# An encoder of two layers in split precision: six seven-product pairs in w_out, five raw slots, an order of its own for each stage's first block

## The chip, the core and the metric

The kernel runs on one core of one Trainium2 chip. The metric is the device time of one execution in microseconds (us); lower is better. Three timed executions of the kernel before gave 2615.0, 2615.23 and 2615.27 us.

The engines are called as the profile calls them: PE (matmuls; PEld its weight loads), DVE (vector), ACT (scalar), POOL and SP. SP issues the loads of the weights, POOL the transfers of intermediate results and those that add to their destination.

## What is computed

The reference is a trunk of two layers over a sequence of 256 tokens of 4096 numbers, in float32. Each layer is

```python
h = rmsnorm(x, norm_w[l])
proj = h @ w_in[l]                      # 4096 x 11264
aq, ak, av, ag, rq, rk, rv, rg = jnp.split(proj, SPLIT_POINTS, axis=-1)
a_out = silu(ag) * gqa_attention(rope(rmsnorm(aq)), rope(rmsnorm(ak)), av)
r_out = silu(rg) * rmsnorm(bidirectional_retention(rope(rq), rope(rk), rv))
x = x + concat([a_out, r_out]) @ w_out[l]   # 4096 x 4096
```

and a last RMSNorm follows. The two projections are nearly all of the arithmetic.

## The kernel before

**Split products.** A float32 number is kept as the sum of two rounded parts, a high one and a low one. A product of two matrices is then three matmuls: high by high, low part of x by high, high by low part of the weight (`M<-whi,x8h`, `M<-whi,x8l` on line 1559, `M<-wlo,x8h` on line 1569). For the weights, ACT makes the high part (`whi<-wraw`, a cast) and DVE the low part (`wlo<-wraw,whi`, a subtraction). All recorded operations of DVE and ACT stand under line 267, a helper's.

**Blocks, pairs and pages.** A projection is done in blocks of 1024 output columns: 11 blocks for w_in and 4 for w_out in each layer. There are four stages: w_in and w_out of layer 0 (stages 0 and 1), then of layer 1 (2 and 3). In a block, the 4096 inputs are 16 pairs of 128-row slices. A pair is a 2 x 2 product of sub-matrices, done either as eight products or, after sums of the sub-matrices, as seven. `SEVENS` (line 85) says which pairs take seven: (3, 4, 6, 10, 11) for w_in and (4, 6, 10, 11, 12) for w_out. A pair of eight has two pages, A and B, each one weight tile of 128 x 1024 with four products. A pair of seven has four, A, T, B and U, with 2, 2, 1 and 2 products: T and U are sums that DVE forms (`wsum`), and B is half a tile (`bhi`, `blo`). Both kinds of pair load two tiles of 512 KB. A pair of seven holds both at once, until its sums and its half page are made.

**Buffers.** Raw weights come into `RAWS` = 6 slots (line 37). High and low parts of whole pages are in a ring of 5 (`RING`), half pages in 2. A load of a raw tile can start when a slot is free, that is, when DVE has read the tile before (`load`, line 483); a page can be cast when PE has released a place in the ring (`release`). 13 pages of 4 KB per partition serve everything else. The operand of x is kept for all 16 pairs: a pair that is ever one of seven has 7 x 128 numbers in `x7h` and `x7l`, the others 2 x 256 in `x8h` and `x8l`.

**Order.** The program is written out ahead by a planner in Python: it emits each engine's instructions in one fixed order, with a clock of its own (`Now`, `Clock`) that prices each operation by constants at the head of the file, and inserts the work between projections (attention, retention, rotary, splitting the next operand) where `Weights.room` (line 641) says that pages are far enough ahead. At run time each engine follows its list and waits on semaphores. Within a block the pairs go 0 to 15 in groups: a group begins with a pair of seven and takes the pairs of eight behind it, whose pages are put between those of the seven (`GROUPS`, `pages_of`). The first block of stage 0 alone has an order of its own, (1, 0, 2, 5, 3, 4, 7, 8, 9, 6, 10, 12, 13, 11, 14, 15), from `SPREAD`. Its pairs 1 and 0 are multiplied unsplit (line 1553) while the first weights come in.

**The end of a block.** Eight sums lie in PSUM; `combine` (line 1576) adds them on DVE into `ca` and `cb`. Where the planner has DVE more than `RELIEF` behind ACT, ACT copies a sum out first (`out`). For w_out the old x is then added by a transfer that accumulates (`ca<-in_x`, `cb<-in_x` on POOL), and the result is transposed for the next layer. The last block of the program has its own ending, `last_combine`.

**Transferred lows.** `far_parts` (line 562) can make a low part without DVE: ACT writes the high part and its negative, and a transfer from memory adds the weight to the negative. `FARS` (line 105) names the pairs whose page B is done so; it is empty before.

Of the kernel before, what the change touches and what calls it, by code (L numbers as in the profile page):

```python
# [14 lines left out]
ALU = mybir.AluOpType  # L15
# [18 lines left out]
BLK = 32  # L34
ALL = slice(None)
PAGES = 13
RAWS = 6

RING = 5
FAR = 1  # L40

STRICT = 9
RELIEF = 0.6
AHEAD = 5
SPARE = 2

HALVES = 2

STEP_V = 1.2
STEP_S = 1.5  # L50

V_FIXED = 0.1
S_FIXED = 0.16
# [2 lines left out]
PASS = 0.3  # L56

LANDING = 9.5
STORE = 5.0
FETCH = 13.0  # L60
FAR_LANDING = 9.0
MARGIN = 0.5

RUSH = 2.5

EARLY = 1.3

ADD_AHEAD = 3.0

NEED = {"ak": 4, "ag": 3, "rk": 5, "rg": 4}  # L70

PE_REST = 1.2

TIGHT_A = 2
TIGHT_B = 9

AT_ONCE = 3

WARM = 20

SPLITS = 1

START = 2

SEVENS = ((3, 4, 6, 10, 11), (4, 6, 10, 11, 12), (3, 4, 6, 10, 11), (4, 6, 10, 11, 12))

EVER = sorted(set(_p for _s in SEVENS for _p in _s))
EIGHTS = [_p for _p in range(NP) if _p not in EVER]
# [7 lines left out]
TAIL = (6, 5, 4)  # L96
LASTS = 2

HOLD = 4

NEAR = 40

LATE = 10

FARS = ((), (), (), ())


AQ, AK, AV, AG, RQ, RK, RVO, RG = 0, 2048, 2560, 3072, 5120, 6144, 7168, 9216
# [65 lines left out]
GROUPS = [  # L174
    ([tuple(range(_s[0]))] if _s[0] else []) + [tuple(range(_a, _b)) for _a, _b in zip(_s, _s[1:] + (NP,))] for _s in SEVENS
]
SPREAD = (4, 5, 9, 10, 13)
FIRST_ORDER = [1, 0] + [_p for _p in range(2, NP) if _p not in SEVENS[0]]
for _i, _p in zip(SPREAD, SEVENS[0]):
    FIRST_ORDER.insert(_i, _p)  # L180
FIRST_GROUPS = []
for _p in FIRST_ORDER:
    if _p in SEVENS[0] or not FIRST_GROUPS:
        FIRST_GROUPS.append(())
    FIRST_GROUPS[-1] += (_p,)
SHARED = ("M1", "M5", "M7", "M6")


# [39 lines left out]

TOGETHER = 4

OTHER = False

TURNS = "01"

# [47 lines left out]
def hybrid_encoder(  # L282
# [134 lines left out]
    class Weights:  # L417


        def __init__(self):  # L420
            self.pages = []
            for l in range(DEPTH):
                for w, n in ((w_in, N_IN), (w_out, N_OUT2)):
                    for b in range(n):
                        stage = 2 * l + (w is w_out)
                        start = (l, b) == (0, 0) and w is w_in
                        for g in FIRST_GROUPS if start else GROUPS[stage]:
                            for slot in slots_of(g, stage, start):
                                one = Page()
                                one.pair, one.kind, one.uses, one.left = slot[0][1], slot[0][3], len(slot), 3 * len(slot)  # L430
                                one.whole = start and one.pair in NATIVE
                                one.seven = one.pair in SEVENS[stage] and not one.whole
                                one.far = False
                                one.can = is_far(stage, one.pair, one.kind) and not (
                                    start and (one.pair < 6 or one.whole)
                                )
                                one.src, one.begun, one.low_at, one.next = [], False, None, []
                                one.kept, one.half = None, one.seven and one.kind == PAGE_B
                                one.allowed = one.wanted = False
# [325 lines left out]
    def split_operand(c, stage, rest=0.0):  # L765
        v, full[c] = full[c], None
        for k in range(2):
            p = 2 * c + k
            whole = None
            if stage == 0:  # L770
                whole = v.rearrange("p (k i n) -> p k i n", k=2, i=2)[:, k]
                w = v.rearrange("p (k i m a t) -> p k m i a t", k=2, i=2, m=MT, t=BLK)[:, k]
            else:
                w = v.rearrange("p (a m i t) -> p m i a t", a=4, m=MT, t=BLK)[:, :, 2 * k : 2 * k + 2]
            waiting.append(Lane(split_pair(p, w, whole, stage)))
            waiting[-1].pair, waiting[-1].ready = p, now.t + rest
        if stage == 0:
            waiting.sort(key=lambda v: (v.pair in NATIVE and not c, FIRST_ORDER.index(v.pair)))

    def split_late():  # L780
        split_operand(*late.pop(0))
# [74 lines left out]
    using = []  # L856

    spare, taken, window, want, users, last_block = {}, {}, [0, False, 99], [0], set(), [False]
    force = [False]

    def take_bank():

# [73 lines left out]
    def running():  # L936
# [4 lines left out]
            one.append(rest)  # L941
        return one

    def advance():

        clear()
        if not lanes + running():
            if waiting:
                split_step()
                return  # L950
            if turning and turning[0].step(True):
                return
            force[0] = True
        ready = lanes + running()
        force[0] = False
        if not ready:
            now.wait(now.t + 0.5)
            return
        one = min(ready, key=lambda v: v.ready)
        now.wait(one.ready)  # L960
        one.step()
        clear()

    def tick():

        weights.low_parts()
# [456 lines left out]
    def lead(stage):  # L1423

        return 8 * SEVENS[stage][0]

    def block(after_pair, phase, then, first_order=False, order=LAST_ORDER, last=None, hurried=False):

# [5 lines left out]
        flat = []  # L1434
        stage = phase - 1
        rush[0] = RUSH if hurried else 0.0
        for g in FIRST_GROUPS if first_order else GROUPS[stage]:
            for slot in slots_of(g, stage, first_order):
                flat += slot
        want[0] = 2  # L1440
# [58 lines left out]
            return a  # L1499

        opens = max(final[b] for b in SHARED)
        after = lead(then - 1) if then else 0

        def end_product(n, name, p, index, k, h):
            g = pages[p, k]
# [70 lines left out]
    def combine(bank, acc, c):  # L1576
# [15 lines left out]
        elif bank in ("M8", "M3", "M2", "M4"):  # L1592
            to = {"M8": cb[:, 1, :], "M3": cb[:, 0, :], "M2": ca[:, 0, :], "M4": ca[:, 1, :]}[bank]
            v = acc[bank]
            if not last_block[0] and ve.until - max(ac.until, now.t) > RELIEF and held[0] + pledged() < PAGES:
                v = page([P, NB], "out")
                ac.copy(v, acc[bank])
                drop()
            ve.tensor_add(to, to, v)

# [250 lines left out]
    for l, L in enumerate(layers):  # L1851
        for bi, (one, _) in enumerate(BLOCKS):
# [10 lines left out]
            c = block(after, 2 * l + 1, 2 * l + 1 + (bi == N_IN - 1), start)  # L1863
            ready = (lambda i=one[1], L=L: i in L.weights) if one[0] == "rg" else None
            tasks.append(Lane(in_task(L, *one, c), need=NEED[one[0]], own=2, gate=ready))
            if one[0] == "ag":
                users.update((v, l, one[1]) for v in "sv")
                tasks.append(Lane(attention_scores(L, one[1]), need=6, gate=lambda g=one[1], L=L: g in L.rs and now.t >= L.kept and near(LATE)))
# [5 lines left out]
        for n in range(N_OUT2):  # L1874
# [19 lines left out]
            else:  # L1894
                if final:
                    turning.append(Turn(2 * l + 2))
                c = block(after, 2 * l + 2, 2 * l + 2 + (n == N_OUT2 - 1), hurried=n == 0)
                tasks.append(Lane(out_tasks(l, n, c), need=4, own=2))


_INS = [
# [46 lines left out]
```

## Time and profile before

| | |
|---|---|
| timed executions, median | 2615.23 us (2615.0 to 2615.27) |
| profiled execution, its own time | 2615.02 us |
| its span, first to last instruction | 2613.2 us |
| outside the span | 1.8 us |
| granted clock of PE, mean | 0.998 |
| weight loads by SP | 956 of 512 KB |

The profile's page gives each engine's busy time. Views of the trace give instructions in order of time, the waits with what ended them, and the chain of work that ended last. The matmuls overlap in the record, so that one shows 389 ns while the next begins 227 ns after it: the pace is read from the starts, not from the durations. For DVE and ACT too the start of the next instruction in a full stretch tells what one costs.

### The profile page before, as it was taken

How to read it: one execution, taken by the hardware profiler on the slowest of the kernel's cores; microseconds unless marked ns; L12 is line 12 of the kernel's file. 1: busy time of each engine (PE TensorE's matmuls, PEld its weight loads, DVE VectorE, ACT ScalarE, POOL GpSimd, SP SyncE). 2: the span in 40 equal slices, each digit the busy share in tenths (PEclk: the TensorE clock that was granted, in tenths of full speed). 3: DMA queues.
4: the chain of work that ended last, by engine and by line, in shares of the span. 5: the costliest groups of instructions: out<-in, count | busy, mean ns of one | idle time of the engine just before them, and what ended most of it. 6: DMA issues, size and time to landing. Idle time of an engine off the chain costs nothing.

```text
span 2613.2 us, 33651 instructions
## 1 busy us (share of the span) xinstructions
PE 2599.5 (99%) x11650; PEld 2152.7 (82%) x11650; DVE 2283.5 (87%) x2715; ACT 1636.4 (63%) x2376; POOL 238.6 (9%) x368
## 2 busy tenths in 40 slices
PE   9999999999999999999999999999999999999998
PEld 7888888888888888888888888888888888888886
DVE  7998988998888998778998889988988798988777
ACT  7765766666555687555785566675665557765454
POOL 0010211111001000110001101210100010000000
PEclk9999999999999999999999999999999999999999
DMA  7876867876666666786777768777765676667774
GB/s 281 297 246 234 274 224 246 278 230 225 205 212 213 238 209 205 238 274 223 260 228 233 223 233 274 244 232 263 253 225 179 223 232 226 198 205 221 231 243 167
DMA packets 180667, 610.47 MB, mean 234 GB/s; under 512 B 21904, under 2 KB 28560, under 8 KB 180496
## 3 DMA queue, kind: packets, MB, share of 16 engines
q1 hardware_dynamic: 147040, 520.17, 59.4%
q0 software_dynamic: 32736, 87.05, 11.1%
q8 instruction: 91, 1.49, 0.2%
q10 hardware_dynamic: 720, 1.10, 0.1%
q14 instruction: 80, 0.66, 0.1%
HBM read 564.20 MB, written 44.04 MB: 233 GB/s over the span
## 4 chain that ended last, share of the span: by engine, by line
PE 97%; DVE 1%; issue 1%; ACT 1%; DMA 1%; SPq 0%; POOLq 0%; DVEq 0%; POOL 0%; ACTq 0%
PE M L1559 62%; PE M L1569 31%; PE M L1042 1%; PE M L1041 1%; PE M L1040 1%; PE M L1553 0%; DVE wlo L267 0%; DMA wraw<-in_w_in 0%; DMA whole<-in_w_in 0%; ACT whi L267 0%; DVE wsum L267 0%; DVE cb L267 0%; ACT ca L267 0%; DVE ca L267 0%; DVE x7l L267 0%
## 5 line engine op out<-in xcount | busy, mean ns | idle before, releaser
L267 ACT CAST whi<-wraw 128x1024 fp32r<-128x1024 f32 x806 | 835.5, 1047 | 555.8 <-PE M L1559 490.5
L267 DVE TENSOR_TENSOR wlo<-wraw,whi 128x1024 fp32r<-128x1024 f32 x806 | 965.2, 1214 | 129.5 <-ACT whi L267 127.5
L1559 PE MATMUL M<-whi,x8h 128*128 128x512 f32 x2368 | 922.1, 389 | 0.0
L1559 PE MATMUL M<-whi,x8l 128*128 128x512 f32 x2368 | 921.7, 389 | 0.0
L1569 PE MATMUL M<-wlo,x8h 128*128 128x512 f32 x2368 | 679.3, 389 | 0.0
L1559 PEld LDWEIGHTS M<-whi,x8h 128*128 128x128 f32 x2368 | 444.6, 188 | 92.1 <-issue 0.2
L1559 PEld LDWEIGHTS M<-whi,x8l 128*128 128x128 f32 x2368 | 444.6, 188 | 92.0 <-issue 0.2
L1569 PEld LDWEIGHTS M<-wlo,x8h 128*128 128x128 f32 x2368 | 442.8, 188 | 90.8
L267 ACT CAST whi<-wsum 128x1024 fp32r<-128x1024 f32 x300 | 315.5, 1052 | 227.9 <-DVE wsum L267 115.3
L1559 PE MATMUL M<-whi,x7h 128*128 128x512 f32 x1140 | 443.6, 389 | 0.0
L1559 PE MATMUL M<-whi,x7l 128*128 128x512 f32 x1140 | 443.5, 389 | 0.0
L267 DVE TENSOR_TENSOR wlo<-wsum,whi 128x1024 fp32r<-128x1024 f32 x300 | 365.5, 1218 | 27.0 <-ACT whi L267 26.6
L1569 PE MATMUL M<-wlo,x7h 128*128 128x512 f32 x1140 | 341.3, 389 | 0.3 <-DVE wlo L267 0.3
L1569 PEld LDWEIGHTS M<-wlo,x7h 128*128 128x128 f32 x1140 | 213.8, 188 | 45.2 <-DVE wlo L267 0.7
L1559 PEld LDWEIGHTS M<-whi,x7h 128*128 128x128 f32 x1140 | 214.0, 188 | 44.9 <-issue 0.4
L1559 PEld LDWEIGHTS M<-whi,x7l 128*128 128x128 f32 x1140 | 214.0, 188 | 44.4
L267 DVE TENSOR_TENSOR wsum<-wraw 128x1024 f32<-128x1024 f32 x150 | 182.4, 1216 | 1.5 <-DMA wraw<-in_w_in 1.5
L267 DVE TENSOR_TENSOR wsum<-wsum,wraw 128x512 f32<-128x512 f32 x150 | 103.8, 692 | 5.2
L267 DVE TENSOR_TENSOR wsum<-wraw,wsum 128x512 f32<-128x512 f32 x150 | 102.5, 684 | 0.6
L267 DVE TENSOR_TENSOR blo<-wraw,bhi 128x512 fp32r<-128x512 f32 x150 | 102.7, 685 | 0.0
L267 ACT CAST bhi<-wraw 128x512 fp32r<-128x512 f32 x150 | 92.3, 615 | 0.0
L267 DVE TENSOR_TENSOR cb<-cb,M 128x512 f32<-128x512 f32 x85 | 58.0, 682 | 37.5 <-PE M L1569 37.4
(223 smaller groups left out, 1876.6 us busy)
## 6 DMA issues: line engine op xcount, KB each, us to landing
wraw<-in_w_in SPq DMA_DIRECT2D x700, 512.0 KB, 4.5
wraw<-in_w_out SPq DMA_DIRECT2D x256, 512.0 KB, 4.2
full<-next_dram POOLq DMA_DIRECT2D x18, 512.0 KB, 7.4
kv<-kv_dram POOLq DMA_DIRECT2D x16, 512.0 KB, 7.0
p_dram<-room POOLq DMA_DIRECT2D x64, 128.0 KB, 3.6
pT<-p_dram POOLq DMA_DIRECT2D x16, 512.0 KB, 8.6
next_dram<-room POOLq DMA_DIRECT2D x40, 128.0 KB, 4.9
x<-in_x SPq DMA_DIRECT2D x8, 512.0 KB, 6.6
```

The costliest lines, as they stand in the source:

```text
L267: return call(out, *args, **kwargs)
L1040: nc.tensor.matmul(out, a[0], b[0], start=start, stop=False)
L1041: nc.tensor.matmul(out, a[0], b[1], start=False, stop=False)
L1042: nc.tensor.matmul(out, a[1], b[0], start=False, stop=stop)
L1559: nc.tensor.matmul(acc[name], a[i], g.hi[h], start=m == first[name] and not i, stop=False)
L1569: nc.tensor.matmul(acc[name], a, g.lo[h], start=False, stop=m == final[name])
```

## The change

- w_out takes seven products for pairs (4, 6, 7, 10, 11, 13), six in place of five; w_in keeps its five. Since a pair of x has its form for all stages, 7 tiles of `x7h` and `x7l` are held, and 9 of `x8h` and `x8l` (before 6 and 10).
- `RAWS` goes from 6 to 5.
- Each stage's first block has an order of its own (`opening_order`, `FIRST_GROUPS[stage]`). Stage 0: (1, 0, 2, 3, 4, 5, 7, 6, 8, 9, 12, 13, 10, 14, 11, 15). Stage 1: (0, 1, 2, 3, 5, 4, 6, 8, 7, 9, 10, 12, 11, 14, 13, 15). Stage 2: 0 to 15 as before. Stage 3: (0, 1, 2, 3, 5, 4, 6, 7, 8, 9, 10, 12, 11, 14, 13, 15).
- `FARS` names pair 15 in stage 1, pair 15 in stage 2, pairs 1 and 2 in stage 3. The planner uses nine of the pages: four in stage 1, two in stage 2, three in stage 3, each with a transfer `flo<-in_w_out` or `flo<-in_w_in` on POOL.
- `OTHER` = True: for the last two column blocks of a layer the transposed result goes to a page of its own (`to`).
- New values for the planner's constants. `ADDED` = 99 leaves the new transfer in `combine` unused.

```diff
-RAWS = 6
+RAWS = 5
...
-RELIEF = 0.6
-AHEAD = 5
-SPARE = 2
+RELIEF = 1.0
+ADDED = 99
+AHEAD = 4
+SPARE = 5
...
-STEP_S = 1.5
+STEP_S = 1.1
...
-STORE = 5.0
-FETCH = 13.0
-FAR_LANDING = 9.0
-MARGIN = 0.5
-RUSH = 2.5
+STORE = 7.0
+FETCH = 9.0
+FAR_LANDING = 10.0
+MARGIN = 0.8
+RUSH = 0.0
...
-ADD_AHEAD = 3.0
-NEED = {"ak": 4, "ag": 3, "rk": 5, "rg": 4}
+ADD_AHEAD = 1.5
+NEED = {"ak": 4, "ag": 3, "rk": 4, "rg": 5}
...
-AT_ONCE = 3
+AT_ONCE = 4
...
-START = 2
-SEVENS = ((3, 4, 6, 10, 11), (4, 6, 10, 11, 12), (3, 4, 6, 10, 11), (4, 6, 10, 11, 12))
+START = 1
+SEVENS = ((3, 4, 6, 10, 11), (4, 6, 7, 10, 11, 13), (3, 4, 6, 10, 11), (4, 6, 7, 10, 11, 13))
...
-HOLD = 4
+HOLD = 8
-LATE = 10
-FARS = ((), (), (), ())
+LATE = 35
+FARS = ((), (15,), (15,), (1, 2))
...
-SPREAD = (4, 5, 9, 10, 13)
-FIRST_ORDER = [1, 0] + [_p for _p in range(2, NP) if _p not in SEVENS[0]]
...
+SPREAD = (3, 4, 7, 12, 14)
+SPREAD1 = (5, 6, 8, 10, 12, 14)
+SPREAD2 = ()
+SPREAD3 = (5, 6, 7, 10, 12, 14)
+def opening_order(stage):
+    spread = (SPREAD, SPREAD1, SPREAD2, SPREAD3)[stage]
+    spread = spread if len(spread) == len(SEVENS[stage]) else SEVENS[stage]
+    order = [_p for _p in ([1, 0] if stage == 0 else [0, 1]) + list(range(2, NP)) if _p not in SEVENS[stage]]
+    for i, p in zip(spread, SEVENS[stage]):
+        order.insert(i, p)
+    return order
...
+FIRST_ORDER = [opening_order(_i) for _i in range(4)]
+FIRST_GROUPS = [grouped(_o, _i) for _i, _o in enumerate(FIRST_ORDER)]
+LEADS = [8 * next(_i for _i, _p in enumerate(_o) if _p in SEVENS[_s]) for _s, _o in enumerate(FIRST_ORDER)]
...
-OTHER = False
+OTHER = True
...
-        for g in FIRST_GROUPS if first_order else GROUPS[stage]:
+        for g in FIRST_GROUPS[stage] if opening else GROUPS[stage]:
...
-        after = lead(then - 1) if then else 0
+        after = 0 if not then else lead(then - 1) if then == phase else LEADS[then - 1]
...
-                c = block(after, 2 * l + 2, 2 * l + 2 + (n == N_OUT2 - 1), hurried=n == 0)
+                c = block(after, 2 * l + 2, 2 * l + 2 + (n == N_OUT2 - 1), opening=n == 0, hurried=n == 0)
```

Two places where the order of instructions moves. The first is DVE in the first block of stage 3 (w_out of layer 1), from the combination of the second retention head into `ca` (the sum in PSUM, M6, times `rst`, which POOL has prepared) on. `wsum` and `wlo` are sums and low parts of weights, `blo` a half page's; equal numbers mean the same tile. Before:

```order
L267 SCALAR_TENSOR_TENSOR ca_19656<-M6_20063,rst_20079,ca_19656 128x256 x2
L267 TENSOR_TENSOR wlo_20093<-wsum_20025,whi_20092 128x1024
L267 TENSOR_TENSOR blo_20096<-wraw_19898,bhi_20095 128x512
L267 STREAM_TRANSPOSE room_20110<-ca_19656 128x1024
L267 TENSOR_TENSOR wlo_20119<-wraw_19962,whi_20118 128x1024
L267 TENSOR_TENSOR wsum_20158<-wraw_19965,wraw_20007 128x1024
L267 TENSOR_TENSOR wlo_20145<-wsum_20087,whi_20144 128x1024
L267 TENSOR_TENSOR wsum_20191<-wraw_19965,wsum_20158 128x512
L267 TENSOR_TENSOR wsum_20191<-wsum_20191,wraw_20007 128x512
L267 TENSOR_TENSOR wlo_20161<-wraw_19965,whi_20160 128x1024
L267 TENSOR_TENSOR wlo_20181<-wraw_20055,whi_20180 128x1024
```

The same place in the changed kernel:

```order
L288 SCALAR_TENSOR_TENSOR ca_19717<-M6_20189,rst_20204,ca_19717 128x256 x2
L288 TENSOR_TENSOR wsum_20224<-wraw_20055,wraw_20072 128x1024
L288 TENSOR_TENSOR wlo_20227<-wraw_20055,whi_20226 128x1024
L288 STREAM_TRANSPOSE room_20236<-ca_19717 128x1024
L288 TENSOR_TENSOR wsum_20244<-wraw_20055,wsum_20224 128x512
L288 TENSOR_TENSOR wsum_20244<-wsum_20244,wraw_20072 128x512
L288 TENSOR_TENSOR wlo_20250<-wsum_20224,whi_20249 128x1024
L288 TENSOR_TENSOR blo_20253<-wraw_20072,bhi_20252 128x512
L288 TENSOR_TENSOR wlo_20267<-wsum_20244,whi_20266 128x1024
L288 TENSOR_TENSOR wsum_20278<-wraw_20099,wraw_20150 128x1024
L288 TENSOR_TENSOR wlo_20281<-wraw_20099,whi_20280 128x1024
L288 TENSOR_TENSOR wlo_20295<-wraw_20160,whi_20294 128x1024
```

Before, one whole page from raw (`wlo_20119`) and the end of an earlier pair of seven stand between the first sums; now a whole pair of seven (pair 6: `wsum_20224` to `wlo_20267`) follows the combination, and the next pair of seven (pair 7, `wsum_20278`) begins right behind it.

The second is POOL at the start of stage 1 (w_out of layer 0), around the last scaling of `rst` and the first transfers that add the old x (`ca<-in_x`, `cb<-in_x`). Before:

```order
L411 TENSOR_TENSOR rst<-rst,half 128x2 x2
L832 DMA full<-next_dram 128x1024 x4
L411 TENSOR_TENSOR rst<-rst,half 128x2 x2
L1667 DMA ca<-in_x 128x2x512
L1667 DMA cb<-in_x 128x2x512
L1644 DMA x_dram<-ca 128x1024
```

In the changed kernel:

```order
L432 TENSOR_TENSOR rst<-rst,half 128x2
L853 DMA full<-next_dram 128x1024 x4
L432 TENSOR_TENSOR rst<-rst,half 128x2 x2
L598 DMA flo<-in_w_out 128x1024
L1700 DMA ca<-in_x 128x2x512
L1700 DMA cb<-in_x 128x2x512
L1677 DMA x_dram<-ca 128x1024
```

One transfer of a low part (`flo<-in_w_out`) now stands on POOL's queue ahead of the transfers that add the old x.

More of the change, by code (lines that the diff above doesn't have):

```diff
@@ L176, with grouped @@
 ]
-SPREAD = (4, 5, 9, 10, 13)
-FIRST_ORDER = [1, 0] + [_p for _p in range(2, NP) if _p not in SEVENS[0]]
[L179 to L185, printed above, removed]
+SPREAD = (3, 4, 7, 12, 14)
[9 more added lines that the diff above has]
+    return order
+def grouped(order, stage):
+    groups = []
+    for p in order:
+        if p in SEVENS[stage] or not groups:
+            groups.append(())
+        groups[-1] += (p,)
+    return groups
+FIRST_ORDER = [opening_order(_i) for _i in range(4)]
+FIRST_GROUPS = [grouped(_o, _i) for _i, _o in enumerate(FIRST_ORDER)]
+LEADS = [8 * next(_i for _i, _p in enumerate(_o) if _p in SEVENS[_s]) for _s, _o in enumerate(FIRST_ORDER)]
 SHARED = ("M1", "M5", "M7", "M6")
@@ L426, in __init__ @@
                         start = (l, b) == (0, 0) and w is w_in
-                        for g in FIRST_GROUPS if start else GROUPS[stage]:
+                        for g in GROUPS[stage] if b else FIRST_GROUPS[stage]:
                             for slot in slots_of(g, stage, start):
@@ L777, in split_operand @@
         if stage == 0:
-            waiting.sort(key=lambda v: (v.pair in NATIVE and not c, FIRST_ORDER.index(v.pair)))
+            waiting.sort(key=lambda v: (v.pair in NATIVE and not c, FIRST_ORDER[0].index(v.pair)))
     def split_late():
@@ L858, in hybrid_encoder @@
     spare, taken, window, want, users, last_block = {}, {}, [0, False, 99], [0], set(), [False]
-    force = [False]
+    force, landing = [False], []
     def take_bank():
@@ L942, in running, with landed @@
         return one
+    def landed():
+        while landing and landing[0] <= now.t:
+            landing.pop(0)
+            drop()
     def advance():
+        landed()
         clear()
@@ L964, in tick @@
     def tick():
+        landed()
         weights.low_parts()
@@ L1425, in lead, with block @@
         return 8 * SEVENS[stage][0]
-    def block(after_pair, phase, then, first_order=False, order=LAST_ORDER, last=None, hurried=False):
+    def block(after_pair, phase, then, first_order=False, opening=False, order=LAST_ORDER, last=None, hurried=False):
         flat = []
@@ L1594, in combine @@
             v = acc[bank]
-            if not last_block[0] and ve.until - max(ac.until, now.t) > RELIEF and held[0] + pledged() < PAGES:
+            busy = ve.until - max(ac.until, now.t)
+            if not last_block[0] and busy > RELIEF and held[0] + pledged() < PAGES:
                 v = page([P, NB], "out")
                 ac.copy(v, acc[bank])
+                if busy > ADDED and ac.until < now.t + 2.0:
+                    nc.gpsimd.dma_start(to, v, accum_op=ALU.add)
+                    landing.append(ac.until + LANDING)
+                    return
                 drop()
@@ L1862, in hybrid_encoder @@
                 turning.append(Turn(2 * l + 1))
-            c = block(after, 2 * l + 1, 2 * l + 1 + (bi == N_IN - 1), start)
+            c = block(after, 2 * l + 1, 2 * l + 1 + (bi == N_IN - 1), start, bi == 0)
             ready = (lambda i=one[1], L=L: i in L.weights) if one[0] == "rg" else None
             tasks.append(Lane(in_task(L, *one, c), need=NEED[one[0]], own=2, gate=ready))
+            tasks[-1].ready = max([0.0] + landing)
             if one[0] == "ag":
@@ L1896, in hybrid_encoder @@
                     turning.append(Turn(2 * l + 2))
-                c = block(after, 2 * l + 2, 2 * l + 2 + (n == N_OUT2 - 1), hurried=n == 0)
+                c = block(after, 2 * l + 2, 2 * l + 2 + (n == N_OUT2 - 1), opening=n == 0, hurried=n == 0)
                 tasks.append(Lane(out_tasks(l, n, c), need=4, own=2))
+                tasks[-1].ready = max([0.0] + landing)
 _INS = [
```

## The prediction

> **What bounds the kernel now.** First the page's busy times, then the chain of work that ended last, then what PE waited for.
>
> ```profile
> span 2613.2 us, 33651 instructions
> PE 2599.5 (99%) x11650; PEld 2152.7 (82%) x11650; DVE 2283.5 (87%) x2715; ACT 1636.4 (63%) x2376; POOL 238.6 (9%) x368
> PE 97%; DVE 1%; issue 1%; ACT 1%; DMA 1%; SPq 0%; POOLq 0%; DVEq 0%; POOL 0%; ACTq 0%
> ```
>
> ```profile
> PE M L1812 <- DVE half L267: 1.1, 1, 1.1
> PE M L1569 <- DVE wlo L267: 0.3, 1, 0.3
> PE M L1553 <- DMA whole<-in_w_in: 0.3, 1, 0.3
> ```
>
> The reader is to see that PE is the chain: 97% of it. In the whole span PE waited 1.7 us, of which 1.1 belongs to the ending (L1812 is in the last combination), 0.3 to the first load and 0.3 to DVE. So a matmul taken out is worth its full pace, and nothing else of the change can gain more than the few tenths that PE waits; but each edit can cost, as DVE at 87% and the loads run close behind PE.
>
> The one wait for DVE stands in the last block of stage 0; the step from the matmul before it is 0.69 us (944.22 to 944.91):
>
> ```profile
> 944.22 0.39 PE L1559 MATMUL M<-whi,x7l 128*128 128x512 f32 x1
> 944.91 0.73 PE L1569 MATMUL M<-wlo,x7h 128*128 128x512 f32 x2 [0.29 <-DVE wlo L267]
> ```
>
> **The products removed.** The pace, from two rows of the chain:
>
> ```profile
> 361.05 1.81 PE M L1559 x8
> 362.87 0.91 PE M L1569 x4
> 363.77 1.81 PE M L1559 x8
> ```
>
> 12 matmuls from 361.05 to 363.77 are 2.72 us, 0.2267 each; the step of 0.69 above is thus 0.46 too long. One pair more takes seven products in each of w_out's four blocks, in two layers: 8 products of 3 matmuls, 24 matmuls of 128x512. The order of PE has 24 fewer, and no other kind changes. 24 x 0.2267 = **−5.44 us**.
>
> (The Trainium skill, page "TensorE: Matmul & The Clock Gate", section "Back-to-back issue gap", gives some 131 ns per matmul of 512 columns in sustained flow. By it the term would be −3.1 us and the time some 2612.4. The rows, at 227 ns, disagree, and decide.)
>
> **What DVE gets for it.** The operations of one pair of seven, first and the one behind the last (7 between the two starts):
>
> ```profile
> 2566.63 1.22 DVE L267 TENSOR_TENSOR wsum<-wraw 128x1024 f32<-128x1024 f32 x1
> ...
> 2573.10 1.22 DVE L267 TENSOR_TENSOR wsum<-wraw 128x1024 f32<-128x1024 f32 x1
> ```
>
> That is 6.47 us, against 21 x 0.2267 = 4.76 us of PE for the same pair: DVE falls 1.7 us behind in each, and makes it up in pairs of eight (two `wlo`, 2.28 us, against 5.44). In the ordinary blocks of w_out three sevens stood in a row before (10, 11, 12), after it two at most (6, 7 and 10, 11): the longest run is shorter, so I cost this at 0. Over the program DVE gains 8 x (6.47 − 2.28) = 33.5 us and loses nine lows, 9 x 1.14 = 10.3: +23 us, while some 330 us of its span are idle (2613.2 less 2283.5). If that cover were gone, see rival E.
>
> **The opening of stage 3.** Here the new order puts pairs 4, 6, 7, all seven, behind each other while retention still runs. What this place looks like before:
>
> ```profile
> 2273.82 0.29 DVE L267 TENSOR_TENSOR xf<-xf,ca 128x128 f32<-128x128 f32 x1
> ...
> 2274.75 0.42 DVE L267 TENSOR_TENSOR x7l<-ca,x7h 128x256 fp32r<-128x256 f32 x1
> 2275.09 1.22 DVE L267 TENSOR_TENSOR wlo<-wraw,whi 128x1024 fp32r<-128x1024 f32 x1
> 2276.22 0.82 DVE L267 TENSOR_TENSOR x7l<-xf,x7h 128x640 fp32r<-128x640 f32 x1
> 2276.96 0.16 DVE L267 TENSOR_SCALAR rst<-rst 128x2 f32<-128x2 f32 x1
> 2277.03 1.22 DVE L267 TENSOR_TENSOR wsum<-wraw 128x1024 f32<-128x1024 f32 x1
> 2278.85 0.87 DVE L267 SCALAR_TENSOR_TENSOR ca<-M,rst,ca 128x256 f32<-128x256 f32 x2 [0.60 <-POOL rst L411]
> 2279.64 1.22 DVE L267 TENSOR_TENSOR wlo<-wraw,whi 128x1024 fp32r<-128x1024 f32 x1
> 2280.77 0.75 DVE L267 TENSOR_TENSOR x8l<-ca,x8h 128x256 fp32r<-128x256 f32 x2
> 2281.44 1.22 DVE L267 TENSOR_TENSOR wlo<-wraw,whi 128x1024 fp32r<-128x1024 f32 x1
> ...
> 2286.68 1.24 DVE L267 STREAM_TRANSPOSE room<-ca 128x1024 f32<-128x1024 f32 x1
> 2287.84 1.18 DVE L267 TENSOR_TENSOR wlo<-wraw,whi 128x1024 fp32r<-128x1024 f32 x1
> ```
>
> ```profile
> 2272.69 0.28 PE L1040 MATMUL M<-vh,wTh 128*128 128x256 f32 x1
> ...
> 2274.00 0.28 PE L1042 MATMUL M<-vh,wTl 128*128 128x256 f32 x1
> ```
>
> In the order of the changed kernel, PE has 107 matmuls of 512 columns and 12 of 256 between the last product of the first retention head and the first use of the low part of pair 7's page A. At 0.2267, and 0.119 for the narrow ones (11 steps from 2272.69 to 2274.00), that is 24.26 + 1.43 = 25.7 us. DVE must do in that time: two whole pairs of seven (4 and 6), 2 x 6.47; the sum and low of page A of pair 7, 2 x 1.14; two more `wlo`, 2.28; the operands, x7l for two pairs, 2 x (0.34 + 0.74), with four `xf` 0.93 and two x8l 0.67; `rst` 0.08 twice; two combinations, 0.79 each; one transpose, 1.16. Sum 24.15 us. POOL's part between `rst` and the combination took 1.9 us from DVE's row to DVE's row (2276.96 to 2278.85). The first time `wsum` and `wlo` cover it; the second time only an x7l of 0.74 does, so DVE waits about 1.0 us: 25.15. That leaves 0.55 us, less than one `wlo`, which DVE may have in hand when the head ends. **Value +0.3 us, ends 0 and +1.5** (that `wlo` whole, and as much again for the wait). Stage 1's opening is like it, but pair 8, an eight, stands between 6 and 7 there: 0.
>
> **The opening of stage 0.** Pair 3, a seven, now follows pair 2.
>
> ```profile
> 25.69 0.39 PE L1559 MATMUL M<-whi,x8h 128*128 128x512 f32 x1
> ...
> 31.13 0.39 PE L1559 MATMUL M<-whi,x7h 128*128 128x512 f32 x1
> ```
>
> ```profile
> 21.45 1.22 DVE L267 TENSOR_TENSOR wsum<-wraw 128x1024 f32<-128x1024 f32 x1
> 22.59 1.22 DVE L267 TENSOR_TENSOR wlo<-wraw,whi 128x1024 fp32r<-128x1024 f32 x1
> ```
>
> Before, PE reached its first seven at 31.13, 5.44 us (one pair of eight) behind 25.69; now it reaches it at 25.69. Before, its first sum began at 21.45 and the low of its page A ended at 23.81; the low is now needed after four matmuls, at 26.6, so even at the old times page A would be there. Ahead of its next sums DVE now has two `wlo`, one x8l, four `xf` and two x7l fewer: 2.28 + 0.67 (an estimate: two of half the size in the rows of stage 3) + 0.93 + 1.08 = 5.0 us, against the 5.44 that PE is earlier. **Value 0, ends 0 and +0.8** (the 0.4 that is lacking, once for each of the two sevens there, 3 and 4).
>
> **Transferred lows.** Nine `wlo` of 1.14 us go to nine transfers.
>
> ```profile
> ca<-in_x POOLq DMA_DIRECT2D x4, 512.0 KB, 8.5
> cb<-in_x POOLq DMA_DIRECT2D x4, 512.0 KB, 12.7
> ```
>
> These are the nearest rows: POOL's transfers of 512 KB that add to their destination land 8.5 us after issue, the second of two 12.7. The shortest stretch of PE between an issue's last condition and the low's use is 74 matmuls, 16.8 us. Behind them on POOL's queue stand the same `ca` and `cb`, which wait for DVE's combination anyway. 0; if the cover went, 12.7 + 8.5 − 16.8 = +4.4 once. ACT makes the negatives and 18 more `out` copies, some 20 us, and is busy 63%: 0. The ending (1.1 above) has the same order behind the last matmul: 0. The wait at 944.91 I keep: 0, or −0.46.
>
> **Five raw slots.**
>
> ```profile
> L488 SPq DMA_DIRECT2D wraw<-in_w_in x700: 327/328/1278, 3.1 to 2242.2; - x175
> L488 SPq DMA_DIRECT2D wraw<-in_w_out x256: 327/328/1135, 949.6 to 2577.3; - x128
> ...
>   PE M L1559: 490.5, 366
> ...
>   DMA wraw<-in_w_in: 26.3, 14
> ...
> DMA to landing us min/median/max: 3.1/4.4/10.3
> ```
>
> 956 loads from 3.1 to 2577.3 are one in 2.69 us. A slot comes round in 6 x 2.69 = 16.2 us, with five in 13.5: each load starts 2.7 us later against its use. Of the 13.5, 4.4 go to landing and up to 6.5 to a seven's sums; 2.6 are left. The rows say that work on raw tiles waited 366 times for PE to give back a place (490.5 us, 1.34 each) and only 14 times for a landing. Raw tiles mostly lie ready; the shift eats the lead and not the pace. **Value 0; ends 0 and +2.7** for each place where a landing becomes the last wait.
>
> **The sum.** Profiled execution 2615.02 (2613.2 of span and 1.8 around it), −5.44 + 0.3 = 2609.88. The median, 2615.23, is 0.21 above it: **2610.1**. 0.2%, about what a measurement of this kernel can tell, is 5.23 us: the bound to "faster" is 2610.0, just beside the forecast.
>
> **Rivals.**
>
> A, the forecast: 24 matmuls go and PE waits up to 1.8 us more at the openings: 2609.8 to 2611.6. Chance 0.55, of which 0.25 under 2610.0.
>
> B, nothing is late and the 0.46 at 944 goes with the new constants: 2609.3, with the wait for the first load 2609.0. For it: DVE's idle 330 us. Against: the new constants aim at no single place. 0.15.
>
> C, one or two loads come late by a slot's 2.7 us: 2610.1 + 2.7 to 2610.1 + 5.4, 2612.8 to 2615.5. For it: the 2.6 us of slack above, and two of five slots held by a seven. Against: the 366 waits for PE. 0.17.
>
> D, slower: five slots starve PE. The mechanism is SP's queue: a load waits until DVE has read a slot's last tile, so two sevens in a row hold four of five slots, and the next pair's first tile starts only when the first seven's last sum is done. Price 2.7 us at each such place; the gain is eaten from the second on, and slower by 0.2% it is from the fourth ((5.23 + 5.44) / 2.7). The six ordinary blocks of w_out have sevens behind each other at 6, 7 and at 10, 11, twelve places; with six of them in full: 2610.1 + 16.2 = 2626. Against: sevens stood three in a row before, and PE's only wait was 0.3. 0.08.
>
> E, DVE becomes the bound. Its +23 us go to the time: 2615.2 + 23 = 2638. For it: 87% busy. Against: PE's 0.3 us of waiting for it. 0.03. (The Trainium skill, page "Perfetto Trace Analysis", section "Identifying the Most-Contended Engine", judges TensorE by the share of its weight loads and not of its matmuls. By it, 82% against 87%, DVE were the engine to spare. The trace disagrees: PE's waits name PE.)
>
> F, the 24 matmuls are worth less than their pace, since they overlap in the record (one shows 0.39 us, the next begins 0.227 behind it): with half of it hidden, −2.7 and 2612.8. Against: PE's rows go at 0.227 throughout. 0.02. (The Trainium skill's figure cited above, page "TensorE: Matmul & The Clock Gate", would have it so.)
>
> **How the numbers follow.** Faster: A's 0.25 and B's 0.15, 0.40. Slower: D and E, 0.11. The rest of A, C and F, 0.49, is within 0.2%. The range goes from B's lower end, 2609.0, to C's upper, 2616.0 with half a us for the spread of both; it leaves out D and E.
>
> **What would show it.** PE's count must fall by 24, and PE's last matmul by about 5.4 us. A wait of PE for `wlo` near the low of pair 7, in stage 3's first block, shows the +0.3. A wait of PE for `whi` or `wlo` behind a cast that waits for a landing of `wraw` is C, many of them D, at the second seven of a row; waits for `wlo` with DVE busy through are E. More waits for landings than 14 with none reaching PE would say that the slots had lead to spare. Wrong I should be if PE waits at a place that I gave 0: the far lows, the `out` copies, the start.

## The result, and the profile after

Over 18 runs of each, the changed kernel takes 2610.35 us (median; 2609.72 to 2611.66) and the kernel before 2615.07 (2614.4 to 2616.17): 4.7 us less, a ratio of 0.9982 with a 95% interval of 0.9975 to 0.9988. The forecast was 2610.1. The profiled execution took 2610.07 us, 2608.3 of it span.

The page after, its busy times and the chain that ended last:

```profile
span 2608.3 us, 33705 instructions
...
PE 2594.4 (99%) x11626; PEld 2148.7 (82%) x11626; DVE 2300.9 (88%) x2754; ACT 1667.7 (64%) x2421; POOL 247.6 (9%) x377
...
PE 98%; DVE 1%; DMA 0%; issue 0%; POOL 0%; SPq 0%; ACT 0%; POOLq 0%; DVEq 0%
```

What PE waited for, after (line, who, us in total, times, longest):

```profile
PE M L1845 <- DVE half L288: 1.1, 1, 1.1
PE M L1581 <- DMA whole<-in_w_in: 0.7, 1, 0.7
PE M L1597 <- DVE wlo L288: 0.3, 1, 0.3
```

24 matmuls fewer, PE still the chain, and hardly a wait: it looks as if nothing but the products had moved. That DVE has 39 instructions more and 17 us more busy time (the prediction had 23) doesn't show on PE. The raw tiles tell otherwise; what the instructions on them waited for (us, times):

```profile
  PE M L1587: 367.7, 284
...
  DMA wraw<-in_w_in: 82.1, 62
  DMA wraw<-in_w_out: 25.2, 17
...
DMA to landing us min/median/max: 3.1/4.5/11.1
```

Waits for a landing rose from 16 (14 for w_in, 2 for w_out) to 79, from some 30 us to 107. The lead of the loads is nearly spent, and still PE pays almost nothing.

Where PE does pay can be listed whole, by steps between starts that are longer than the pace. Right behind the first split product both kernels have one (0.63 us before, 0.64 after). Later, before, only the place at 944 had such a step. After there are three, none of them at 944, always ahead of the low part of a pair of seven's page A: in the last blocks of stages 0 and 2, and in the first block of stage 3:

```profile
914.37 0.39 PE L1587 MATMUL M<-whi,x7l 128*128 128x512 f32 x1
915.01 0.74 PE L1597 MATMUL M<-wlo,x7h 128*128 128x512 f32 x2 [0.25 <-DVE wlo L288]
915.59 0.40 PE L1587 MATMUL M<-whi,x7h 128*128 128x512 f32 x1
```

```profile
2207.71 0.39 PE L1587 MATMUL M<-whi,x7l 128*128 128x512 f32 x1
2208.13 0.73 PE L1597 MATMUL M<-wlo,x7h 128*128 128x512 f32 x2
2208.70 0.39 PE L1587 MATMUL M<-whi,x7h 128*128 128x512 f32 x1
```

```profile
2301.51 0.39 PE L1587 MATMUL M<-whi,x7l 128*128 128x512 f32 x1
2301.90 0.73 PE L1597 MATMUL M<-wlo,x7h 128*128 128x512 f32 x2
2302.47 0.39 PE L1587 MATMUL M<-whi,x8h 128*128 128x512 f32 x1
```

From the first row to the last of each are three steps, 0.68 us at pace; the rows are 1.22, 0.99 and 0.96 apart. So PE loses 0.54 (before, at 944, 0.58), 0.31 and 0.28 us. Two of the three have no releaser printed: short waits hide in the starts. PE's last matmul began at 2600.88 before:

```profile
2600.88 0.39 PE L1569 MATMUL M<-x7l,x8h 128*128 128x512 f32 x1
```

and now begins at

```profile
2596.01 0.39 PE L1597 MATMUL M<-x7l,x8h 128*128 128x512 f32 x1
```

That is −4.87 us, and the sum closes: −5.44 for the products, +0.03 at the first split product, −0.04 at the end of stage 0, +0.31 at that of stage 2, +0.28 at the opening of stage 3, −4.86. The tail behind the last matmul is 12.3 us in both.

### The profile page after: what moved, and what is told of

Read it like the earlier page. It is cut to its first block, busy times and chain, and to the rows that moved or that the text cites. A ratio compares the mean times of both kernels' runs of the same rounds, so it can differ in the third digit from the quotient of the medians.

```text
span 2608.3 us, 33705 instructions
## 1 busy us (share of the span) xinstructions
PE 2594.4 (99%) x11626; PEld 2148.7 (82%) x11626; DVE 2300.9 (88%) x2754; ACT 1667.7 (64%) x2421; POOL 247.6 (9%) x377
## 4 chain that ended last, share of the span: by engine, by line
PE 98%; DVE 1%; DMA 0%; issue 0%; POOL 0%; SPq 0%; ACT 0%; POOLq 0%; DVEq 0%
PE M L1587 63%; PE M L1597 31%; PE M L1070 1%; PE M L1069 1%; PE M L1068 1%; PE M L1581 0%; DVE wlo L288 0%; DMA whole<-in_w_in 0%; DMA wraw<-in_w_in 0%; DVE ca L288 0%; DVE cb L288 0%; DVE x8l L288 0%; POOL rst L432 0%; DVE room L288 0%; SPq L544 0%
## 5 line engine op out<-in xcount | busy, mean ns | idle before, releaser
L1587 PE MATMUL M<-whi,x8h 128*128 128x512 f32 x2092 | 814.8, 389 | 0.0
L1587 PE MATMUL M<-whi,x8l 128*128 128x512 f32 x2092 | 814.4, 389 | 0.0
L1597 PE MATMUL M<-wlo,x8h 128*128 128x512 f32 x2092 | 599.4, 389 | 0.0
L1587 PE MATMUL M<-whi,x7h 128*128 128x512 f32 x1364 | 530.6, 389 | 0.0
L1587 PE MATMUL M<-whi,x7l 128*128 128x512 f32 x1364 | 530.6, 389 | 0.0
L1587 PEld LDWEIGHTS M<-whi,x8l 128*128 128x128 f32 x2092 | 392.9, 188 | 81.1 <-issue 0.2
L1587 PEld LDWEIGHTS M<-whi,x8h 128*128 128x128 f32 x2092 | 392.9, 188 | 81.0 <-ACT whi L288 0.2
L1597 PEld LDWEIGHTS M<-wlo,x8h 128*128 128x128 f32 x2092 | 391.7, 188 | 80.8 <-DVE wlo L288 0.2
L1597 PE MATMUL M<-wlo,x7h 128*128 128x512 f32 x1364 | 406.0, 389 | 0.3 <-DVE wlo L288 0.3
L1587 PEld LDWEIGHTS M<-whi,x7l 128*128 128x128 f32 x1364 | 256.1, 188 | 53.2
```

The lines of the kernel that those rows point to most:

```text
L1587: nc.tensor.matmul(acc[name], a[i], g.hi[h], start=m == first[name] and not i, stop=False)
L1597: nc.tensor.matmul(acc[name], a, g.lo[h], start=False, stop=m == final[name])
```

## The experiments

Two theories were tried against each other. "Products only": the whole gain is 24 matmuls, and slots, orders, transferred lows and constants move less than 0.5 us each. "Arrangement": the gain is only to be had with them. Each run is set beside runs of the kernel before on the same chip (medians of 2615.1 to 2615.2). Each time is the median of 11 executions (e4, e8 and e9 of 4, e10 of 5).

**e1: the changed kernel without the new products.**

```diff
-SEVENS = ((3, 4, 6, 10, 11), (4, 6, 7, 10, 11, 13), (3, 4, 6, 10, 11), (4, 6, 7, 10, 11, 13))
+SEVENS = ((3, 4, 6, 10, 11), (4, 6, 10, 11, 12), (3, 4, 6, 10, 11), (4, 6, 10, 11, 12))
```

> The changed kernel with the old pairs of seven in w_out (4, 6, 10, 11, 12): five slots, the orders of stage 0, transferred lows, own pages and constants stay; the own orders of stages 1 and 3 fall away with the pairs. Theory 'products only' (all of the gain is 24 matmuls at 0.2267 us, the rest moves less than 0.5 us): 2615.0 to 2615.8, that is before within 0.5. Rival 'arrangement' (orders, transferred lows and constants bring part of the gain): below 2614.0.

Measured 2616.2 us, ratio 1.0004 (0.9995 to 1.0013). The rival falls in this form: without the products, what is left of the change gains nothing (the own orders of stages 1 and 3, made for six pairs, are not in this kernel). The theory's range ended at 2615.8; the 1.0 us over the kernel before lies within the interval.

**e2: the new products without the rest.** The kernel before with the six pairs of seven and `RAWS = 5`.

```diff
-RAWS = 6
+RAWS = 5
...
-SEVENS = ((3, 4, 6, 10, 11), (4, 6, 10, 11, 12), (3, 4, 6, 10, 11), (4, 6, 10, 11, 12))
+SEVENS = ((3, 4, 6, 10, 11), (4, 6, 7, 10, 11, 13), (3, 4, 6, 10, 11), (4, 6, 7, 10, 11, 13))
```

> The kernel before with two edits: the six pairs of seven in w_out and five raw slots (its memory holds no sixth beside them); the order of stages 1 and 3 is plain, no lows are transferred, constants are old. Theory 'products only': PE's sum falls by 5.44 us and some waits come back at the openings of stages 1 and 3, 2609.8 to 2612.5. Rival 'arrangement': the gain is not to be had without the orders and transferred lows, 2613.0 or more.

Measured 2615.4 us, ratio 1.0001 (0.9992 to 1.001). "Products only" falls. PE has 24 matmuls fewer, and the time of before: its last matmul begins at 2600.79, 0.09 us earlier, so 5.35 of the 5.44 us are lost again on the way.

```profile
PE M L1569 <- DVE wlo L267: 1.6, 4, 0.5
...
PE M L1559 <- DVE x8l L267: 0.6, 1, 0.6
```

By the steps between starts, 1.8 us of it are lost at the end of stage 0 and 1.7 at the end of stage 2, over what was lost there before, and 1.2 near 1378 in the first block of stage 2, where PE waits for `x8l`; the rest goes in steps too small to list. The openings of stages 1 and 3, where the theory looked for waits, have no long step.

**e3: five slots alone.** The kernel before with `RAWS = 5`.

> The kernel before with five raw slots in place of six and nothing else. Theory 'slots eat lead, not pace': 2615.0 to 2615.6, with casts and sums that wait for a landing rising from 16 to 50 or more and PE waiting under 1 us more. Rival 'slots cost' (a late load reaches PE at one place or more, 2.7 us each): 2617.7 or more.

Measured 2619.7 us, ratio 1.0016 (1.0007 to 1.0025), 4.5 us slower. The rival holds in size, but not in form: no single late load of 2.7 us reaches PE. Waits for a landing rise from 16 to 88. PE's waits in the split products, all near the ends of stages 0 and 2:

```profile
PE M L1569 <- DVE wlo L267: 1.6, 4, 0.5
...
PE M L1559 <- ACT whi L267: 0.8, 2, 0.6
...
PE M L1559 <- DVE cb L267: 0.3, 1, 0.3
```

How they come about stands in one stretch of DVE in the last block of stage 0. The kernel before, then with five slots; the order of the operations is the same:

```profile
909.32 0.75 DVE L267 TENSOR_TENSOR x8l<-full,x8h 128x256 fp32r<-128x256 f32 x2
909.98 1.22 DVE L267 TENSOR_TENSOR wsum<-wraw 128x1024 f32<-128x1024 f32 x1
```

```profile
907.17 1.24 DVE L267 STREAM_TRANSPOSE room<-ca 128x1024 f32<-128x1024 f32 x1
...
909.43 0.75 DVE L267 TENSOR_TENSOR x8l<-full,x8h 128x256 fp32r<-128x256 f32 x2
911.60 1.23 DVE L267 TENSOR_TENSOR wsum<-wraw 128x1024 f32<-128x1024 f32 x1 [1.42 <-DMA wraw<-in_w_in]
```

The sum waits 1.42 us for a landing. That landing is late for two reasons. With six slots the tile was loaded at 893.54; with five its load is issued at 903.08. And there it takes 8.4 us to land, where the median is 4.4: POOL has issued four fetches of 512 KB just ahead, and the 16 DMA engines are full (the share behind the clock of 1.00, then GB/s):

```profile
900.97 2.18 POOL L832 DMA_DIRECT2D full<-next_dram  x4
```

```profile
903.08 4.53 SPq L488 DMA_DIRECT2D wraw<-in_w_in  x4
```

```profile
908.00:913.00 5.00, 5.00 (x24) 4.14 (x23) 3.58 (x6) 0.17 (x1) 0.00 (x0) 1.00 1.01 407
```

From there to the end of the block DVE has no idle time but behind ACT, 3.6 us in all against 3.4 before, and ACT none but behind DVE, so they can't make the delay up. It reaches PE 15 to 35 us later, in pieces:

```profile
926.21 0.61 PE L1569 MATMUL M<-wlo,x7h 128*128 128x512 f32 x2
927.39 0.50 PE L1559 MATMUL M<-whi,x8h 128*128 128x512 f32 x1 [0.57 <-ACT whi L267]
...
942.02 0.73 PE L1569 MATMUL M<-wlo,x7h 128*128 128x512 f32 x2 [0.51 <-DVE wlo L267]
```

By the first row of retention in the next block, PE is 1.75 us later than it was ahead of this stretch, against the kernel before; the last block of stage 2 adds 2.65, most of it behind landings of 7.5 to 8.7 us that follow four such fetches, and outside these two places and the first loads (0.1) no row of PE moves.

**e4: four slots.** The changed kernel with `RAWS = 4`.

> The changed kernel with four raw slots. A slot then comes round in 4 x 2.7 = 10.8 us, and landing (4.5) with the sums of a pair of seven (6.5) takes 11.0, so two sevens behind each other cannot be fed in time. Theory 'lead is spent': slower than the changed kernel, somewhere from 2615 to 2700 (some 60 such places at 0 to 2.7 us, less what eights between them give back), 2640 as the middle. Rival 'slots never matter, PE is the bound': within 1 us of the changed kernel, 2610 to 2611.

Measured 2665.05 us, ratio 1.019 (1.0176 to 1.0204). 310 waits for a landing, 482 us:

```profile
  DMA wraw<-in_w_in: 316.7, 220
  DMA wraw<-in_w_out: 165.7, 90
```

The fifth slot is worth 55 us in the changed kernel. With four, a round of the slots is estimated at 10.8 us, against 11.0 for a landing and a pair of seven's sums, as was worked out ahead of the run, and the landing is late all over the span, not at two places.

**e5: no transferred lows.** `FARS = ((), (), (), ())`.

> The changed kernel with no transferred lows: DVE makes the nine low parts (10.3 us more of DVE work, most of it in the first blocks of stages 1 to 3). Theory 'products only': the wait for a low at the openings grows by at most one low part each, 2610.0 to 2611.5. Rival 'arrangement' (the transfers carry DVE over the openings): 2612.0 or more.

Measured 2610.61 us, ratio 0.9984 (0.9975 to 0.9993). The theory holds: between the medians the nine transfers bring 0.3 us, which is within the spread.

**e6: stages 1 and 3 opened in plain order.** `SPREAD1 = SPREAD3 = ()`.

> The changed kernel with pairs 0 to 15 in plain order in the first blocks of stages 1 and 3 (pair 4, a seven, comes one earlier, then 6, 7). Theory 'products only': PE waits for a low at two openings, up to 1.1 us each, 2610.3 to 2612.5. Rival 'arrangement': 2613.0 or more.

Measured 2613.55 us, ratio 0.9994 (0.9985 to 1.0003). The rival holds: beside the new constants, the two own orders are worth 3.2 us of the 4.7. In the rows of the profiled execution each of the two openings loses some 1.5 us. In e2, with the old constants and no transferred lows, the same plain orders show no long step there: what an order is worth hangs on what stands beside it. The longest waits stand in the first blocks of stages 1 and 3. In stage 1:

```profile
1006.76 0.40 PE L1597 MATMUL M<-blo,x7h 128*128 128x512 f32 x1
1007.74 0.49 PE L1587 MATMUL M<-whi,x7h 128*128 128x512 f32 x1 [0.58 <-ACT whi L288]
```

The same moment on ACT:

```profile
1004.96 1.65 ACT L288 COPY ca<-room 32x256 f32<-32x256 f32 x4
1006.63 1.05 ACT L288 CAST whi<-wsum 128x1024 fp32r<-128x1024 f32 x1
```

PE waits for the high part of a pair of seven's sum, and ACT makes it late because it copies a transposed head out first (`ca<-room`). At 2302 in stage 3 the rows repeat, with the same 0.58.

**e7: pair 8 between 6 and 7 in stage 3.**

```diff
-SPREAD3 = (5, 6, 7, 10, 12, 14)
+SPREAD3 = (5, 6, 8, 10, 12, 14)
```

> The changed kernel with stage 3 opened as stage 1: pair 8, an eight, stands between the sevens 6 and 7. The term of the prediction (+0.3 us for the low of pair 7's page A, a gap of 0.28 near 2301.8 in the trace) would go: 2610.0 to 2610.1, and no gap there. Rival: DVE is behind there whatever the order, the gap moves to another seven and the time stays at 2610.35 or rises.

Measured 2609.91 us, ratio 0.9981 (0.9972 to 0.999). The step at 2301.5 is gone; pair 6's low is followed by an eight at pace:

```profile
2301.47 0.62 PE L1597 MATMUL M<-wlo,x7h 128*128 128x512 f32 x2
2301.92 0.39 PE L1587 MATMUL M<-whi,x8h 128*128 128x512 f32 x1
```

The fastest kernel of the study, though 0.44 us is within the intervals. The rows carry the step, not the time: in the profiled execution the last matmul begins at 2596.13, 0.12 us later than in the changed kernel, since the first split products begin 0.24 later and the step at 2208 is 0.18 longer.

**e8: a seventh pair of seven in w_out.**

```diff
-SEVENS = ((3, 4, 6, 10, 11), (4, 6, 7, 10, 11, 13), (3, 4, 6, 10, 11), (4, 6, 7, 10, 11, 13))
+SEVENS = ((3, 4, 6, 10, 11), (3, 4, 6, 7, 10, 11, 13), (3, 4, 6, 10, 11), (3, 4, 6, 7, 10, 11, 13))
...
-SPREAD1 = (5, 6, 8, 10, 12, 14)
+SPREAD1 = ()
...
-SPREAD3 = (5, 6, 7, 10, 12, 14)
+SPREAD3 = ()
```

> The changed kernel with one more pair of seven in w_out: pairs 3, 4, 6, 7, 10, 11, 13 (every pair that has a form for seven), stages 1 and 3 opened in plain order. Another 24 matmuls of 128x512 go. Theory 'products only': 5.44 us less again, plus 0.3 to 2.5 us of waits at the openings, 2605.2 to 2607.5. Rival 'DVE is the bound by then' (another 33 us for DVE): 2609.0 or more.

Measured 2642.21 us, ratio 1.0104 (1.009 to 1.0118). The rival, and far beyond it (the plain openings alone cost 3.2 us in e6). DVE is the bound, but only in the opening blocks of stages 1 to 3: there it splits the operand beside the weights, and PE waits for `x7l` and the retention's `ca`. In the ordinary blocks of w_out no step of PE is longer than the pace. Constants chosen for seven pairs were not tried.

```profile
PE M L1587 <- DVE x7l L288: 17.3, 8, 5.4
PE M L1587 <- DVE ca L288: 5.8, 2, 2.9
```

**e9 and e10: a sixth slot for a page.** The kernel of e2, and that of e7, with

```diff
-RAWS = 5
-PAGES = 13
+RAWS = 6
+PAGES = 12
```

> The kernel before with the six pairs of seven and six raw slots; the sixth slot takes the place of one of the 13 pages of 4 KB. With five slots this was 2615.4, and five slots alone cost the kernel before 4.5 us. Revised theory 'late landings at the ends of stages 0 and 2 pay the gain back': with six slots those waits go, 2610.5 to 2611.5, and what is left above 2609.8 are the plain openings. Rival 'the page was worth as much as the slot' (fewer sums copied out by ACT, waits elsewhere): 2613 or more.

> The changed kernel with pair 8 between 6 and 7 in stage 3 (2609.91 before this edit) and a sixth raw slot in place of one of 13 pages. Theory 'the two waits left, 0.54 us near 914 and 0.5 near 2208, come from late landings': they go, 2609.0 to 2609.4. Rival 'pages are what the new constants live on': 2610.5 or more, with PE waiting for DVE or ACT at another place.

Measured 2750.47 us, ratio 1.0517 (1.0502 to 1.0531), and 2691.29, ratio 1.0291 (1.0277 to 1.0305). Neither tells of the slots. With one page fewer the planner begins attention's last task only in the first block of w_out. The four gates of attention take turns in two places in memory, and in both kernels the fourth gate is stored (`g_dram<-room`, at 444 us) before the second has been fetched (`sgT<-g_dram`, at 526 us in e9 and 465 in e10). So a part of attention is multiplied by another part's gate, and the result is not the reference's. PE waits 14 us at once (`pTh`) in both. Whether a sixth slot beside 13 pages would win the last waits stays open: memory has no room for both.

**e11: old constants.** The changed kernel with the planner's constants of before, `RELIEF` to `AT_ONCE`, `START`, `HOLD`, `LATE`, among them

```diff
-AHEAD = 4
-SPARE = 5
+AHEAD = 5
+SPARE = 2
...
-NEED = {"ak": 4, "ag": 3, "rk": 4, "rg": 5}
-AT_ONCE = 4
+NEED = {"ak": 4, "ag": 3, "rk": 5, "rg": 4}
+AT_ONCE = 3
```

> The changed kernel with the old values of the planner's constants (RELIEF to AT_ONCE, START, HOLD, LATE); the six pairs of seven, five slots, own orders, transferred lows and own pages stay. Theory 'the constants place the work between projections so that a late landing does not reach PE': the waits of the run with five slots alone come back in the last blocks of stages 0 and 2, 1.7 and 2.0 us, 2613.0 to 2614.5. Rival 'the orders and transferred lows do it': 2610.2 to 2611.0.

Measured 2618.07 us, ratio 1.0011 (1.0003 to 1.002). The theory's mechanism holds, and its price is larger: 7.7 us more than the changed kernel, and 2.7 more than e2, which has these constants with plain orders. The steps of e3 are back, near 929, 944 and 949 and near 2224, 2239 and 2244, and with them others: at the start, in attention, in the opening of stage 3.

```profile
PE M L1597 <- DVE wlo L288: 2.0, 5, 0.5
PE M L1587 <- DVE cb L288: 1.4, 2, 0.9
PE M L1587 <- ACT whi L288: 1.3, 2, 0.7
```

What the new constants do to the stretch that broke in e3 can be seen in the changed kernel's own DVE:

```profile
899.78 1.24 DVE L288 STREAM_TRANSPOSE room<-ca 128x1024 f32<-128x1024 f32 x1
...
908.20 1.23 DVE L288 TENSOR_TENSOR wsum<-wraw 128x1024 f32<-128x1024 f32 x1 [2.55 <-DMA wraw<-in_w_in]
```

This is the same sum. DVE waits longer for the landing, 2.55 us, but the landing itself comes 3.4 us earlier. The transposition that ends a retention head stands 7 us earlier and POOL's four fetches 3.2, at 897.79, so that the load lands 5.9 us after its issue and not 8.4 (in e11, with the fetches at 903.77, it is 8.0). DVE is ahead when it begins to wait, and PE loses 0.54 us in this stretch, where with five slots alone its long steps come to 2.3. Whether the earlier fetches alone would do it was not tried.

**e12: only the old prices.** The changed kernel with seven of these constants old:

```diff
-STEP_S = 1.1
+STEP_S = 1.5
...
-STORE = 7.0
-FETCH = 9.0
-FAR_LANDING = 10.0
-MARGIN = 0.8
-RUSH = 0.0
+STORE = 5.0
+FETCH = 13.0
+FAR_LANDING = 9.0
+MARGIN = 0.5
+RUSH = 2.5
...
-ADD_AHEAD = 1.5
+ADD_AHEAD = 3.0
```

> The changed kernel with the old values of the seven constants that price an operation or a transfer in the planner's clock (STEP_S, STORE, FETCH, FAR_LANDING, MARGIN, RUSH, ADD_AHEAD); the limits (RELIEF, AHEAD, SPARE, NEED, AT_ONCE, START, HOLD, LATE) stay new. With all of them old the changed kernel lost 7.7 us. Theory 'prices': they decide where work between projections stands, so most of that comes back, 2614.5 or more. Rival 'limits': they decide how many tasks run at once and how many pages are kept, so little comes back, 2610.3 to 2612.0; between these both have a part.

Measured 2612.58 us, ratio 0.999 (0.9981 to 0.9999): 2.2 us of the 7.7. Between theory and rival; the larger part belongs to the limits (how many tasks at once, how many pages kept), or to limits and prices together. Which of the eight limits matter was not tried, nor were stage 0's own order and `OTHER` taken back alone.

## Why the forecast was right, and which of its reasons were not

**The products: right.** −5.44 us was forecast, and PE's last matmul comes 4.87 earlier, with the difference accounted for by steps in the rows.

**The opening of stage 3: right in place and size.** +0.3 forecast for the low of pair 7's page A; 0.28 measured at that row, and gone with pair 8 put between (e7). The terms differ, and their sum agrees: the wait of DVE for POOL's `rst` that the working put at about 1.0 us was 0.59, in the row below; DVE waited 0.33 more for a high part, and had 0.6 of earlier work in hand when the head ended, where the working allowed up to 1.14.

```profile
2291.10 0.88 DVE L288 SCALAR_TENSOR_TENSOR ca<-M,rst,ca 128x256 f32<-128x256 f32 x2 [0.59 <-POOL rst L432]
```

**The opening of stage 0, the transferred lows, the tail: right at 0.** 0.03 at the first split product, no wait for a `flo` in the changed kernel, 0.3 us between the medians without them (e5), the same 12.3 us of tail.

**The wait at 944: the right number by luck.** It was kept in the sum. But it went, and another of like size came at 914, where a sum waits 2.55 us for a landing: 0.54 for 0.58.

**Five slots: the right sum from a wrong reason.** "Raw tiles mostly lie ready; the shift eats the lead and not the pace" is true of most blocks and false of two places. In the changed kernel they show as the 0.54 at 914 and the 0.31 at 2208, behind sums that wait 2.55 and 2.01 us for a landing. With nothing else changed, five slots cost 4.5 us (e3), more than the 0 that was put in, and rival C's price was right for the wrong mechanism: not a load of 2.7 us that reaches PE, but 1.4 us that DVE can't make up. The step that failed is reading the cushion from figures of the whole span: 366 waits for PE against 14 for landings, and the median landing of 4.4 us. With the 8.4 us of the load that was late, the prediction's own sum, 13.5 less 6.5 less the landing, lacks 1.4 us where it had 2.6 left. The places that decide are the two in which landings are slow and DVE and ACT have nothing to give up, and there the average says nothing.

**The constants: not priced at all.** They got one clause, "the new constants aim at no single place", and the value 0. They are worth 7.7 us in the changed kernel (e11), more than the products; the two own orders are worth 3.2 (e6), where the prediction spoke only of what they might cost. The two figures are not shares of one sum, since each part was taken back beside the other: constants, orders, transferred lows and own pages together bring 5 us, from e2 to the changed kernel. Put together: the products give 5.4, the sixth slot given up for them costs 4.5 (e3), the two at once leave the time where it was (e2), and the rest wins the 5. The forecast of the sum came out since the changed kernel as a whole leaves PE almost without waits, which is what its values of 0 said. That a cost and a gain of like size, both put at 0, cancel is luck.

**The rivals.** B did not come: the place at 944 went quiet, but three others cost 1.13 us. D did not come, but its mechanism is real one slot further down: 310 waits and 55 us (e4). E did not come; with a seventh pair it does, in the opening blocks, with these constants and plain openings (e8). F fell: the removed matmuls are worth their full pace.

## What to carry to other kernels

A buffer's depth is priced where landings are slow and the engines that drain it have no time to give up, not by the mean wait over the span: look for the stretch where other transfers fill the DMA engines, take the landing of that stretch and not the median, and ask what a landing 1 to 3 us later does there. A change that takes work from the bound and memory from the buffers may give nothing by itself (e2) and everything once the order of the side work is set anew; so undoing one part alone shows what that part protects, not what it brings. And a wait printed at 0.25 us, or not printed, may be 0.3 to 0.5 in the starts: compare starts with the pace.

## What the runs showed of the hardware

In e8 a long wait of PE costs twice. PE waits 2.92 us, and the matmuls behind it start 0.43 us apart and not 0.227, for 3 us:

```profile
988.50 0.39 PE L1587 MATMUL M<-whi,x7l 128*128 128x512 f32 x1
991.81 0.80 PE L1587 MATMUL M<-whi,x7h 128*128 128x512 f32 x1 [2.92 <-DVE ca L288]
...
994.54 0.63 PE L1597 MATMUL M<-blo,x7h 128*128 128x512 f32 x1
994.96 0.48 PE L1587 MATMUL M<-whi,x7h 128*128 128x512 f32 x1
```

After the wait of 5.4 us at 1032.57, the granted clock is 0.50 from 1038 to 1045 (the third number from the end), and 0.93 in the mean of the 10 us behind it:

```profile
1020.00:1032.00 12.00, 11.54 (x51) 9.23 (x50) 11.93 (x17) 8.01 (x12) 0.00 (x0) 1.00 0.69 226
...
1038.00:1045.00 7.00, 5.98 (x13) 4.33 (x14) 6.52 (x9) 3.85 (x5) 0.37 (x1) 0.50 0.60 187
1045.00:1055.00 10.00, 10.00 (x42) 8.15 (x42) 6.18 (x7) 6.25 (x9) 0.55 (x1) 0.93 0.89 260
```

So of the 39 us that PE loses in e8 (its last matmul 28.6 us later than before, with 48 matmuls fewer, 10.9), the waits are 23.1; most of the other 16 are matmuls at half the clock. The shorter waits of e4, 2.2 us at the longest, leave the clock at full speed (0.999 in the mean).

The Trainium skill, page "TensorE: Matmul & The Clock Gate", section "What's actually happening", has the clock halved after at least one idle window of some 3.4 us. The halving agrees with these rows; the wait that was enough here was 2.92 us.
